# The first sum of weight blocks moves from VectorE to GpSimd, and ten steps of sixteen take seven products

## The chip, the cores and the metric

The kernel runs on one core of one Trainium2 chip. The metric is the time on the device, in microseconds (us), of one execution. PE is TensorE, DVE VectorE, ACT ScalarE, POOL GpSimd and SP SyncE. A "mixed unit" below is the piece of work that repeats 17 times in the kernel and that the change edits.

## The reference

With the sizes used here (sequence 256, width 4096, 32 heads of 128, one layer) the program is an attention branch and a final norm:

```python
h = x + attn_branch(rms_norm(x, norm_attn), w_in_attn, w_out_attn)
return rms_norm(h, final_norm)

def attn_branch(xn, w_in, w_out):
    proj = xn @ w_in                       # (256, 4096) @ (4096, 16384)
    q, k, v, g = jnp.split(proj, 4, axis=-1)
    o = stick_breaking_attention(to_heads(q), to_heads(k), to_heads(v))
    return (o * jax.nn.silu(g)) @ w_out    # (256, 4096) @ (4096, 4096)
```

Nearly all the arithmetic lies in the two products with `w_in` and `w_out`, in float32. The convolution branch of the reference file is not reached at this depth.

## The kernel before

**Products in three matmuls.** A float32 operand is split into a high part (rounded to the matmul's input form) and a low part (what is left). A product of two 128 x 128 by 128 x 512 operands is made of three matmuls into one PSUM bank: high by high, high by low, low by high. The weight tiles arrive by DMA into `raw` tiles (seven buffers); ACT casts a block to its high part `wh`, DVE subtracts it and leaves the low part `wl`. These two are made afresh for each block, since every weight is used once. Five buffers of two blocks and two of one block hold `wh` and `wl` between DVE and PE.

**Units and steps.** The output columns are worked off in units of four 512-column pieces (two row halves by two column groups). 15 of the 16 units over `w_in` and two of those over `w_out` are mixed units; the others (one plain unit of each matrix, and two single ones at the end) multiply in the plain way. A unit has 16 steps over the contraction; each step takes a 2 x 2 block of 128-row weight pieces against a 2 x 2 block of the input.

**Seven or eight products.** In a mixed unit a step whose number stands in `SEVEN` (line 42) uses a Strassen-Winograd scheme of seven products on seven forms of weights; the other steps use eight plain products. `SEVEN_PARTS` and `EIGHT_PARTS` (lines 67 and 73) list the parts. An eight-product step casts and splits four blocks (two `wl` rows of 128 x 1024). A seven-product step splits seven (three `wl` rows of 128 x 1024 and one of 128 x 512), because it also needs sums of weight blocks. One of these, called T3 in the code, is made by a DMA that adds while it writes (`add_block`, line 401, issued by POOL). The other three are made by `sums(q)` (line 424), in place in the two raw tiles `one` and `two`: `one0 = one0 - two0`, then `two1 = one0 + two1`, then `one1 = one0 + one1`. All three are `TENSOR_TENSOR` rows of 128 x 512 on DVE: in the rows of the order the first reads `raw_0<-raw_0,raw_1`, the second `raw_1<-raw_0,raw_1` and the third `raw_0<-raw_0`. The first waits until T3 has landed and the first part's `wl` is made from the old contents; the second waits also for the single-block part.

**Order.** Each engine runs its instructions in the order of the program, and this order is fixed when the program is built. A planner (`Plan`) walks through all the work with assumed costs; when an engine is free, `turn` (line 212) takes the ready item with the lowest key. Keys are places in the sequence of products (`first[n]` is when part n is first needed, in ns of assumed PE time). DVE's sums have the key of the part that needs them less 3000. POOL issues the adding DMAs, the writes of the heads' outputs to DRAM (`spill`) and the later reloads (`p`). Attention heads of one unit run between the products of the next one: `head` and `gate` add PE transposes and matmuls, ACT functions and DVE rows (`f`, `fl`, `a`, `gated`, `gl`); `combine` adds up the unit's banks on DVE.

All instructions that pass through the planner's engine wrapper are recorded at line 115, so groups are told apart by tile names.

Of the kernel before, what the change touches and what calls it, by code (L numbers as in the profile page):

```python
# [14 lines left out]
ALU = mybir.AluOpType  # L15
# [13 lines left out]
W = 2 * CW  # L29
# [9 lines left out]

SEVEN = (1,3,5,7,8,10,11,13,14)
RAW_BUFS = 7
PAIRS = 5
SINGLES = 2
# [41 lines left out]

def scalar_ns(n):
    return 98 + n / 1.2


def tensor_ns(n):
# [138 lines left out]
def kernel(  # L231
# [10 lines left out]
    nc = Plan(tc)  # L242
# [30 lines left out]
    for u, (kind, w, cols) in enumerate(units):  # L273
        for s in range(NS):
# [5 lines left out]
            else:  # L280
# [6 lines left out]
                else:  # L287
                    which = SEVEN_PARTS if s in (SEVEN) else EIGHT_PARTS
            for i, (k, place, prods) in enumerate(which):
# [24 lines left out]
    starts, ends, first, left, place_of = {}, {}, {}, {}, {}  # L314
# [12 lines left out]
    def place_at(u, s):  # L327

        u, s = u + int(s // NS), s % NS
        a = place_of[u, int(s)]  # L330
        b = place_of.get((u, int(s) + 1), place_of.get((u + 1, 0), a))
        return a + (b - a) * (s - int(s))

    def soon(c=4.0):
        return nc.here + 1e3 * c


    def dve(emit, n, key=None, **kw):
        n = n if isinstance(n, tuple) else (n,)
        cost = sum(vector_ns(m) for m in n) + 122 * (len(n) - 1)  # L340
        return nc.work("vector", cost, emit, soon() if key is None else key, **kw)

    def act(emit, n, key=None, **kw):
        n = n if isinstance(n, tuple) else (n,)
        cost = sum(scalar_ns(m) for m in n) + 100 * (len(n) - 1)
        return nc.work("scalar", cost, emit, soon() if key is None else key, **kw)
# [66 lines left out]
    def tile_done(*tile):  # L413
        tile_left[tile] -= 1
        if not tile_left[tile]:
            nc.give("raw")
# [7 lines left out]
    def sums(q):  # L424

        a, b, c, d = quad_parts[q]
        one, two = raw[q, 0], raw[q, 1]
        for k in range(2):
            tile_left[q, k] += 1

        def add(to, at_, f, g, key, op=ALU.add):
            return dve(
                lambda: nc.vector.tensor_tensor(out=to[:, :, at_, :], in0=f, in1=g, op=op), W,
                key - SUMS_AHEAD * 1e3,
            )

        yield nc.until(("lows", a), ("T3", q))
        yield add(one, 0, one[:, :, 0, :], two[:, :, 0, :], first[c], ALU.subtract)
        yield nc.until(("lows", b))
        yield add(two, 1, one[:, :, 0, :], two[:, :, 1, :], first[c])  # L440
        nc.tell(("sums", c))
        yield add(one, 1, one[:, :, 0, :], one[:, :, 1, :], first[d])
        nc.tell(("sums", d))
        for k in range(2):
            tile_done(q, k)

    def piece(n, c, there):

        p = parts[n]
        yield nc.until(*there)  # L450
        full = raw[p["tile"]][:, :, p["place"], :][:, :, c, :].rearrange("p i c n -> p c i n")
        h, l = (t[n][:, c, :].rearrange("p c (i n) -> p c i n", i=HG) for t in (wh, wl))
        size = (c.stop - c.start) * W
        key = first[n] - (AHEAD * 1e3 if p["seven"] and p["i"] < 2 else 0)
        yield act(lambda: nc.scalar.copy(h, full), size, key - 2.0 * 1e3)
        yield dve(lambda: minus(l, full, h), size, key)
        for k in range(c.start, c.stop):
            nc.tell(("low", n, k))
        low_done(n)

    def split(size, tag, bufs):
        for n, p in enumerate(parts):
            if p["size"] != size:
                continue
            q = p["quad"]
            yield nc.take(tag)
            t = p["tile"][1]
            if q:
                yield nc.until(("raw", q, t))
            wh[n] = wp.tile([P, size, W], F32R, tag=tag + "h", name=f"wh{n}", bufs=bufs)  # L470
            wl[n] = wp.tile([P, size, W], F32R, tag=tag + "l", name=f"wl{n}", bufs=bufs)
            cuts = [slice(k, k + 1) for k in range(KT)] if q == 0 else [slice(0, size)]
            lows_left[n] = len(cuts)
            if p["seven"] and p["i"] == 0:
                nc.start(sums(q))
            for c in cuts:
                if q == 0:
                    there = [("raw", q, t, c.start)]
                else:
                    there = [("sums", n)] if p["seven"] and p["i"] > 1 else [("raw", q, t)]  # L480
                nc.start(piece(n, c, there))
# [7 lines left out]
    def new_forms(i, what):  # L489
        n = len(SEVEN_FORMS if i in SEVEN else EIGHT_FORMS)  # L490
        h = sp.tile([P, n, P], F32R, tag=f"xh{i}", name=f"{what}h{i}")
        l = sp.tile([P, n, P], F32R, tag=f"xl{i}", name=f"{what}l{i}")
        forms[i] = h, l
        return h, l

    def both_parts(i, to, f, key):
        h, l = (t[:, to, :] for t in forms[i])
        n = (to.stop - to.start) * P
        yield act(lambda: nc.scalar.copy(h, f), n, key - 1e3)
        yield dve(lambda: minus(l, f, h), n, key)  # L500

    def sums_of(i, y, what, key):

        tt = nc.vector.tensor_tensor
        if i not in SEVEN:
            y4 = y.rearrange("p (a b) c -> p a b c", a=KT)
# [21 lines left out]
    def blocks_of(i):  # L528
# [8 lines left out]
        if i:  # L537
            yield moved("sync", lambda: nc.sync.dma_start(y, xT[i]), [KT * S], key - 1, hold=True)

            def scaled():  # L540
                for c in range(KT):
                    nc.scalar.activation(y[:, c, :], y[:, c, :], AF.Copy, scale=gain(c))
                nc.scalar.copy(h[:, 0:4, :], y4)

            yield act(scaled, (S, S, 2 * S), key - 2e3)
            yield dve(lambda: minus(l[:, 0:4, :], y4, h[:, 0:4, :]), 2 * S, key)
        else:
            for k in range(KT):
                yield moved("scalar", lambda: nc.scalar.dma_start(y[:, k, :], xT[i][:, k, :]), [S], key - 1,
                            hold=k == 1, after=k == 0 and (lambda: nc.tell("x0")) or None)  # L550
                if k == 0:
                    yield moved("scalar", lambda: nc.scalar.dma_start(gcol, gain_in), [KC], key - 1,
                                after=lambda: nc.tell("gain"))
            for c in range(KT):
                hc, lc = (t[:, 2 * c : 2 * c + 2, :].rearrange("p a b -> p (a b)") for t in (h, l))

                def two_parts():
                    nc.vector.tensor_scalar(out=hc, in0=y[:, c, :], scalar1=gain(c), scalar2=None, op0=ALU.mult)
                    nc.vector.scalar_tensor_tensor(
                        out=lc, in0=y[:, c, :], scalar=gain(c), in1=hc.bitcast(F32), op0=ALU.mult, op1=ALU.subtract  # L560
                    )

                yield dve(two_parts, (S, S), key)
# [25 lines left out]
    for _ in range(WARM):  # L589
# [8 lines left out]
        out=bound, in_=bound, compare_op=ALU.is_gt, fill=0.0, base=0,  # L598
# [6 lines left out]
        out=tri_f, in_=tri_f, compare_op=ALU.is_ge, fill=0.0, base=0, pattern=[[-1, P]], channel_multiplier=1,  # L605
# [321 lines left out]
    def blocks_of_heads(s):  # L927
# [12 lines left out]
        nc.give("gh")  # L940
        if s in SEVEN:
            key = min(place_at(OUT0, s + 1), place_of[OUT0 + 1, s] - 3e3)
# [7 lines left out]
    def again(s):  # L950

        yield nc.until(("used", LAST - 2, s), later_than(LAST - 2, s))
        y = yield from heads_of(s, soon(), slice(1, 2))
        yield from both_parts(s, slice(1, 2), y[:, 1:2, :], soon())
        nc.give("gh")
        nc.tell(("form", "r", s))
# [79 lines left out]
    def blocks_out(u, c):  # L1036

        for d in range(2):
            for t in range(NT):
                yield nc.until(("used", u, 2 * (NT * d + t)), ("C", u - 1))  # L1040
                if t == 0:
                    yield nc.take("gh")
                    yield load_gain(c + d)
                yield nc.take("gh")
                yield load_out(c + d, t)
                yield from block_out(c + d, t, hs[c + d, t])
                nc.give("gh")
            nc.give("gh")
# [110 lines left out]
    def products():  # L1159
        for g, (n, k) in enumerate(order):  # L1160
# [9 lines left out]
            else:  # L1170
                what = "r" if u > LAST - 2 and s in SEVEN else "p"
            if starts[u, b] == (n, k):
# [20 lines left out]
    for k, c in enumerate(range(0, NJ - 2, 2)):  # L1193
        if k:
            nc.start(mixed_h(U + k, c))
        nc.start(blocks_out(U + k + 1, c))
    for s in SEVEN:
        nc.start(again(s))
# [40 lines left out]
```

## Time and profile before

| quantity | value |
|---|---|
| three runs | 1757.85 us median (1756.26 to 1759.46) |
| span of the profiled execution | 1754.0 us |
| mean granted clock of PE | 0.997 |
| busy PE / DVE / ACT / POOL | 1736.9 / 1560.4 / 1166.4 / 295.7 us |
| DMA share in the 40 slices | 4 to 9 tenths, mostly 7 or 8 |
| moved by DMA | 405.86 MB |

For the profiled execution the page gives only the span, from its first to its last instruction. The median of the runs stands 3.85 us above it; this is what lies around the span. Busy times of pipelined engines overlap at the ends of rows, so the busy time of a group is the union of its rows, while the mean of one row is longer than the distance from one start to the next. A wait is written as waiter <- releaser.

### The profile page before, as it was taken

How to read it: one execution, taken by the hardware profiler on the slowest of the kernel's cores; microseconds unless marked ns; L12 is line 12 of the kernel's file. 1: busy time of each engine (PE TensorE's matmuls, PEld its weight loads, DVE VectorE, ACT ScalarE, POOL GpSimd, SP SyncE). 2: the span in 40 equal slices, each digit the busy share in tenths (PEclk: the TensorE clock that was granted, in tenths of full speed). 3: DMA queues.
4: the chain of work that ended last, by engine and by line, in shares of the span. 5: the costliest groups of instructions: out<-in, count | busy, mean ns of one | idle time of the engine just before them, and what ended most of it. 6: DMA issues, size and time to landing. Idle time of an engine off the chain costs nothing.

```text
span 1754.0 us, 24699 instructions
## 1 busy us (share of the span) xinstructions
PE 1736.9 (99%) x7806; PEld 1427.1 (81%) x7806; DVE 1560.4 (89%) x1971; ACT 1166.4 (67%) x1594; POOL 295.7 (17%) x364
## 2 busy tenths in 40 slices
PE   8999999999999999999999999999999999999997
PEld 6888888888888888888888888888888888888885
DVE  7889999999999999999999999999999997899963
ACT  7975767676767676767676767676767675666543
POOL 0012121111111121211111111111112111111100
PEclk9999999999999999999999999999999999999998
DMA  9968777777777878787878787878786877889874
GB/s 340 316 192 224 230 218 229 223 223 226 222 228 217 239 210 239 208 245 210 240 208 245 208 239 206 242 202 245 200 246 200 262 244 239 229 245 271 257 236 156
DMA packets 242867, 405.86 MB, mean 231 GB/s; under 512 B 27520, under 2 KB 67968, under 8 KB 242736
## 3 DMA queue, kind: packets, MB, share of 16 engines
q1 hardware_dynamic: 193968, 352.15, 60.8%
q0 software_dynamic: 47184, 49.76, 17.3%
q10 hardware_dynamic: 1584, 2.38, 0.4%
q8 instruction: 61, 1.00, 0.2%
q14 instruction: 70, 0.57, 0.1%
HBM read 396.05 MB, written 8.13 MB: 230 GB/s over the span
## 4 chain that ended last, share of the span: by engine, by line
PE 92%; DVE 3%; issue 2%; DMA 2%; ACT 1%; SPq 0%; ACTq 0%; DVEq 0%
PE acc L115 87%; PE z L115 2%; DVE wl L115 2%; PE o L115 2%; DMA raw<-in_w_in_dram 1%; PE tr L115 1%; ACT wh L115 1%; DVE raw L115 0%; ACT h L115 0%; SPq L115 0%; DMA xres<-in_x_dram 0%; DMA raw<-in_w_out_dram 0%; ACTq L115 0%; DVE gv_sb L115 0%; DVE h L115 0%
## 5 line engine op out<-in xcount | busy, mean ns | idle before, releaser
L115 ACT CAST wh<-raw 128x1024 fp32r<-128x1024 f32 (+1 forms) x948 | 886.1, 976 | 476.1 <-issue 173.3
L115 DVE TENSOR_TENSOR wl<-raw,wh 128x1024 fp32r<-128x1024 f32 (+1 forms) x948 | 1032.1, 1131 | 125.3 <-ACT wh L115 118.6
L115 PE MATMUL acc<-wh,sh 128*128 128x512 f32 x1913 | 762.6, 399 | 2.4 <-DVE sh L115 2.1
L115 PE MATMUL acc<-wh,sl 128*128 128x512 f32 x1913 | 746.2, 390 | 0.0
L115 PE MATMUL acc<-wl,sh 128*128 128x512 f32 x1913 | 744.9, 389 | 0.8 <-DVE wl L115 0.8
L115 PEld LDWEIGHTS acc<-wh,sh 128*128 128x128 f32 x1913 | 359.4, 188 | 77.3 <-DVE gv_sb L115 3.9
L115 PEld LDWEIGHTS acc<-wh,sl 128*128 128x128 f32 x1913 | 359.1, 188 | 76.9 <-DVE sl L115 0.8
L115 PEld LDWEIGHTS acc<-wl,sh 128*128 128x128 f32 x1913 | 359.7, 188 | 71.5 <-DVE wl L115 1.5
L115 POOL DMA_DIRECT2D raw<-in_w_in_dram x270 | 236.1, 987 | 1075.7 <-DMA raw<-in_w_in_dram 403.1
L115 DVE TENSOR_TENSOR raw<-raw,raw 128x512 f32<-128x512 f32 x306 | 210.3, 687 | 5.1
L115 PE MATMUL acc<-wh,oh 128*128 128x512 f32 x494 | 193.2, 391 | 0.0
L115 PE MATMUL acc<-wl,oh 128*128 128x512 f32 x494 | 192.4, 389 | 0.6 <-DVE wl L115 0.6
L115 PE MATMUL acc<-wh,ol 128*128 128x512 f32 x494 | 192.3, 389 | 0.0
L115 PEld LDWEIGHTS acc<-wl,oh 128*128 128x128 f32 x494 | 92.8, 188 | 20.5 <-DVE wl L115 1.2
L115 PEld LDWEIGHTS acc<-wh,oh 128*128 128x128 f32 x494 | 92.8, 188 | 19.3 <-DVE gv_sb L115 0.4
L115 PEld LDWEIGHTS acc<-wh,ol 128*128 128x128 f32 x494 | 92.7, 188 | 19.2
L115 DVE TENSOR_TENSOR raw<-raw 128x512 f32<-128x512 f32 x153 | 104.5, 683 | 0.0
L115 POOL DMA_DIRECT2D raw<-in_w_out_dram x36 | 31.6, 992 | 132.5 <-DMA raw<-in_w_out_dram 66.2
L115 ACT ACTIVATE f<-f 128x384 f32<-128x384 f32 x96 | 50.5, 526 | 3.0
L115 DVE SCALAR_TENSOR_TENSOR f<-z,f 128x384 f32<-128x384 f32 x32 | 17.8, 557 | 31.2 <-ACT f L115 31.2
L115 POOL DMA_DIRECT2D p<-spill x33 | 20.3, 696 | 129.6 <-DVE ol L115 94.0
L115 ACT ACTIVATE gl<-gl 128x512 f32<-128x512 f32 x48 | 30.0, 625 | 7.3 <-DVE gl L115 7.3
(90 smaller groups left out, 745.9 us busy)
## 6 DMA issues: line engine op xcount, KB each, us to landing
raw<-in_w_in_dram SPq DMA_DIRECT2D x1020, 256.0 KB, 4.6
raw<-in_w_out_dram SPq DMA_DIRECT2D x256, 256.0 KB, 3.9
raw<-in_w_in_dram POOLq DMA_DIRECT2D x270, 128.0 KB, 5.2
raw<-in_w_out_dram POOLq DMA_DIRECT2D x36, 128.0 KB, 5.6
xr<-in_x_dram SPq DMA_DIRECT2D x16, 256.0 KB, 5.2
xres<-in_x_dram SPq DMA_DIRECT2D x16, 256.0 KB, 5.6
xs<-in_xT_dram SPq DMA_DIRECT2D x15, 256.0 KB, 5.3
spill<-gated POOLq DMA_DIRECT2D x15, 256.0 KB, 3.9
```

The costliest lines, as they stand in the source:

```text
L115: return self.tc.keep_in_program_order(getattr(self.engine, name)(*args, **kw))
```

## The change

Two things change. The first of the three sums of a seven-product step is issued on GpSimd by a new helper `pool_add`, with its own assumed cost and a key 25 us ahead of the part that needs it; the second and third sums stay on DVE. And `SEVEN` becomes another set of ten steps instead of nine. The set also decides which of the input's forms are made (seven forms for a step in `SEVEN`, six for another, once per matrix) and which heads are reloaded for them.

```diff
-SEVEN = (1,3,5,7,8,10,11,13,14)
+SEVEN = (1, 2, 4, 5, 7, 8, 10, 11, 13, 14)
...
+def pool_ns(n):
+    return 200 + 2.2 * n
...
+    def pool_add(to, f, g, key, op=ALU.add):
+        return nc.work(
+            "gpsimd", pool_ns(W), lambda: nc.gpsimd.tensor_tensor(out=to, in0=f, in1=g, op=op), key
+        )
...
         yield nc.until(("lows", a), ("T3", q))
-        yield add(one, 0, one[:, :, 0, :], two[:, :, 0, :], first[c], ALU.subtract)
+        yield pool_add(one[:, :, 0, :], one[:, :, 0, :], two[:, :, 0, :], first[c] - 2.5e4, ALU.subtract)
         yield nc.until(("lows", b))
         yield add(two, 1, one[:, :, 0, :], two[:, :, 1, :], first[c])
         nc.tell(("sums", c))
```

The rows of the two programs show what moves. Below is DVE in the seventh mixed unit around its step 8, with the numbers of the tiles: `raw120_0` and `raw120_1` are the two raw tiles of that step, `wl356` in the program before and `wl370` in the changed one are the low part of its first two blocks. Before:

```order
L115 TENSOR_TENSOR wl356_6271<-raw120_0_6142,wh356_6270 128x1024 [waits DMAHW1_49,DMAHW0_49,Activation_49]
L115 TENSOR_TENSOR raw120_0_6142<-raw120_0_6142,raw120_1_6097 128x2x256 [waits DMASW3_49,DMASW2_49,DVE_49]
L115 TENSOR_TENSOR raw120_1_6097<-raw120_0_6142,raw120_1_6097 128x2x256 [waits DVE_49]
L115 TENSOR_TENSOR raw120_0_6142<-raw120_0_6142 128x2x256
L115 TENSOR_TENSOR wl358_6291<-raw120_1_6097,wh358_6290 128x1024 [waits Activation_49]
L115 TENSOR_TENSOR wl359_6302<-raw120_0_6142,wh359_6301 128x1024 [waits Activation_49]
```

And with the change, at the same step:

```order
L119 TENSOR_TENSOR wl370_6346<-raw120_0_6245,wh370_6345 128x1024 [waits DMAHW1_49,DMAHW0_49,Activation_49]
L119 TENSOR_TENSOR raw120_1_6187<-raw120_0_6245,raw120_1_6187 128x2x256 [waits Pool_49]
L119 TENSOR_TENSOR raw120_0_6245<-raw120_0_6245 128x2x256 [waits DVE_49]
L119 TENSOR_TENSOR wl372_6366<-raw120_1_6187,wh372_6365 128x1024 [waits DMASW1_49,DMASW0_49,Activation_49]
L119 TENSOR_TENSOR wl373_6375<-raw120_0_6245,wh373_6374 128x1024 [waits Activation_49]
```

The row between the low part and the second sum is gone from DVE, and the second sum now waits for POOL. The sum on POOL itself cannot start before the low part is done, because it overwrites what that row reads. Of the 170 steps of seven products in the changed program, 41 have no DVE row between the low part and the second sum, 51 have one, 32 two, 31 three and 15 four.

On POOL, for the same stretch (steps 119 to 126 are steps 7 to 14 of that unit; a `DMA raw` row is T3 of that step, in two pieces). Before:

```order
L115 DMA raw119_1_6055<-in_w_in_dram 128x256 x2
L115 DMA raw120_1_6097<-in_w_in_dram 128x256 x2
L115 DMA raw122_1_6192<-in_w_in_dram 128x256 x2
L115 DMA spill6_6265<-gated6_6088 128x512
L115 DMA raw123_1_6276<-in_w_in_dram 128x256 x2
```

With the change:

```order
L119 TENSOR_TENSOR raw119_0_6178<-raw119_0_6178,raw119_1_6118 128x2x256
L119 DMA spill6_6327<-gated6_6141 128x512
L119 DMA raw122_1_6274<-in_w_in_dram 128x256 x2
L119 TENSOR_TENSOR raw120_0_6245<-raw120_0_6245,raw120_1_6187 128x2x256
L119 DMA raw123_1_6348<-in_w_in_dram 128x256 x2
L119 TENSOR_TENSOR raw122_0_6339<-raw122_0_6339,raw122_1_6274 128x2x256
L119 DMA raw125_1_6424<-in_w_in_dram 128x256 x2
L119 TENSOR_TENSOR raw123_0_6400<-raw123_0_6400,raw123_1_6348 128x2x256
L119 DMA raw126_1_6492<-in_w_in_dram 128x256 x2
L119 TENSOR_TENSOR raw125_0_6480<-raw125_0_6480,raw125_1_6424 128x2x256
L119 TENSOR_TENSOR raw126_0_6539<-raw126_0_6539,raw126_1_6492 128x2x256
```

The adding DMAs now stand behind sums that wait for DVE: T3 of step 126 is issued after the sum of step 123, and used two sums later. In the whole program PE has 51 matmul rows of products fewer, DVE 75 rows fewer, ACT 37 rows more, and POOL 170 sums and 36 DMA rows more.

## The prediction

> **What bounds the kernel now.** I read the engines' shares first, then the chain of waits, then the waits by engine, and then the mixed units by windows. The shares and the chain's summary:
>
> ```profile
> PE 1736.9 (99%) x7806; PEld 1427.1 (81%) x7806; DVE 1560.4 (89%) x1971; ACT 1166.4 (67%) x1594; POOL 295.7 (17%) x364
> PE 92%; DVE 3%; issue 2%; DMA 2%; ACT 1%; SPq 0%; ACTq 0%; DVEq 0%
> 654.40 51.03 PE acc L115 x225
> ```
>
> PE carries 92% of the chain. The third line, from the chain in order of time, is a stretch without a break: 225 matmuls start in 51.03 us, one every 0.2268 us. The 389 ns that a row of such a matmul lasts is pipelined and is no price. A product of three matmuls costs 0.680 us.
>
> The view of waits says how near DVE is:
>
> ```profile
> PE acc L115 <- DVE wl L115: 1.4, 2, 0.8
> DVE wl L115 <- ACT wh L115: 118.6, 182, 3.5
> DVE f L115 <- ACT f L115: 31.2, 30, 1.4
> ```
>
> PE hardly ever waits for a low part. DVE's waits for `wh` are those of an engine that is ahead, since ACT's casts wait for buffers that PE frees. The waits in the heads (`f`, 31.2 us over 15 units, 2.1 each) would stay if DVE fell behind.
>
> The windows put numbers on one mixed unit over `w_in` (its length is half of the 173.7 us after which the chain repeats), and on the two over `w_out`:
>
> ```profile
> core 0: us, PE busy (x) PEld busy (x) DVE busy (x) ACT busy (x) POOL busy (x), PEclk, DMA share, GB/s
> 480.72:567.50 86.78, 86.78 (x393) 71.46 (x393) 79.92 (x96) 58.28 (x78) 15.77 (x19) 1.00 0.78 223
> 567.50:654.40 86.90, 86.90 (x395) 71.47 (x394) 80.02 (x96) 58.94 (x79) 16.84 (x20) 1.00 0.79 225
> sum 521.00, PE 520.99 PEld 428.79 DVE 479.82 ACT 351.61 POOL 97.88; mean PE 86.83 PEld 71.47 DVE 79.97 ACT 58.60 POOL 16.31
> sum 160.00, PE 160.00 PEld 132.50 DVE 139.97 ACT 95.57 POOL 29.75; mean PE 80.00 PEld 66.25 DVE 69.98 ACT 47.79 POOL 14.88
> ```
>
> The first sum is of six units, the second of 160 us that cover the two units over `w_out`. PE is full at a granted clock of 1.00. DVE works 79.97 of 86.83 us: 6.9 us of reserve, of which 2.1 are the heads' waits. Over `w_out` it works 70.0 of 80. So PE is the bound, and DVE is the engine that becomes it if its work grows by some 5 us per unit.
>
> **What the change takes from PE.** 17 mixed units lose one product each: 17 x 0.680 = 11.6 us. This is the whole gain if nothing else binds: 86.83 becomes 86.15 per unit.
>
> **What it does to DVE's own work.** The prices:
>
> ```profile
> L115 DVE TENSOR_TENSOR wl<-raw,wh 128x1024 fp32r<-128x1024 f32 x791 | 935.7, 1220 | 120.2 <-ACT wh L115 113.5 <-DMA raw<-in_w_in_dram 2.2 <-DMA xres<-in_x_dram 1.5
> L115 DVE TENSOR_TENSOR raw<-raw,raw 128x512 f32<-128x512 f32 x306 | 210.3, 687 | 5.1
> L115 DVE TENSOR_TENSOR wl<-raw,wh 128x512 fp32r<-128x512 f32 x157 | 107.2, 683 | 5.1 <-ACT wh L115 5.1
> ```
>
> A `wl` row of 1024 takes 935.7/791 = 1.18 us, a sum 0.69, a `wl` row of 512 0.68. Nine first sums leave: -6.2. The tenth step of seven adds one `wl` of 1024, one of 512 and two sums: 1.18 + 0.68 + 1.37 = +3.2. So 79.97 becomes 77.0 us per unit, in 86.15. By work alone DVE is relieved. ACT gets two casts more per unit (under 2 us on 58.6 of 86.8) and the DMA two adding transfers; at shares of 0.67 and 0.79 I cost both at nothing, covered by PE. The input's further forms are made once per matrix, under 4 us of DVE in all, in its reserve.
>
> **What POOL's sum costs.** The trace has no two-input row on POOL. The nearest:
>
> ```profile
> L115 POOL TENSOR_SCALAR_AFFINE_SELECT bound<-bound 128x128 f32<-128x128 f32 x1 | 0.3, 292 | 0.1
> L1226 POOL MEMSET const-bfloat16-1.0<- 128x1 bf16 x1 | 0.1, 101 | 0.0
> L115 POOL DMA_DIRECT2D raw<-in_w_in_dram x270 | 236.1, 987 | 1075.7 <-DMA raw<-in_w_in_dram 403.1 <-DVE raw L115 226.3 <-DVE wl L115 210.2
> ```
>
> 101 ns for one element is the fixed part; 292 - 101 = 191 ns for 128 elements of one input makes 0.76 us for 512, so 0.87 us is the lower end. If two inputs take twice as long per element, 0.10 + 1.53 = 1.63 is the upper. I take the middle, 1.2 us. The Trainium skill (GPSIMD Engine Reference, section 3.1) gives 4497 ns for 2048 elements of a two-input float32 sum, as an estimate 1.1 us for 512; by that figure the forecast below would be 15 us lower.
>
> **What DVE loses by it.** The second sum cannot start before POOL's sum, and POOL's cannot start before the first low part. One row shows the way from DVE to POOL:
>
> ```profile
> 655.76 0.42 DVE L115 TENSOR_TENSOR gated<-o,gated 128x256 f32<-128x256 f32 x1
> 656.48 0.58 POOL L115 DMA_DIRECT2D spill<-gated  x1 [2.29 <-DVE gated L115]
> ```
>
> From 656.18 to 656.48, 0.30 us. So 1.5 us pass from low part to second sum, and what DVE has between them is at most what the order put there: nothing at 41 of the 170 places, one row (0.6 to 1.2 us) at 51. The lower end is that DVE runs those rows at full speed beside POOL: 1.5 less what stands between, averaged over the places of the order with a row of 1024 at 1.13 (the distance of starts) and one of 512 at 0.60, is 6.3 us per ten steps. Then DVE needs 77.0 + 2.1 + 6.3 = 85.4 of 86.15 and PE still binds, by a hair.
>
> The upper end is that nothing of DVE runs while POOL sums, because DVE's rows here are nearly all of two inputs from the same memory that POOL is reading twice. Then each step costs the whole sum: 10 x 1.2 = 12.0, and DVE needs 77.0 + 2.1 + 12.0 = 91.1 us per unit. No row of this trace has a POOL instruction that reads beside a DVE row of two inputs, so the trace doesn't choose. I take the upper end, since the lower one needs two engines with four input streams to run side by side at full speed, and already leaves DVE without reserve. I leave out the 0.30 us where DVE has nothing between, against the few rows with one input from PSUM that might run beside POOL.
>
> The Trainium skill (SBUF — State Buffer, "Who interferes with whom") has a rule that speaks against the change: a vector instruction with two SBUF inputs contends with a GpSimd instruction that reads SBUF, and whichever starts second is blocked until the other ends. By that rule the upper end holds; no run here shows it so far.
>
> **The sum.** Over `w_in`: 91.1 - 86.83 = +4.3 per unit, times 15 = +64. Over `w_out` DVE needs 70.0 - 3.0 + 12.0 = 79.0 of 80 less 0.7: PE still binds, two units gain 1.4. Together +63 on the profiled 1754.0 us, that is 1817 in span and, with the 3.85 us around it, **1820 us** against the median. With the sum at 0.87 us DVE needs 87.8 and the time is 1757.85 + 15 x 1.0 - 1.4 = 1772; at 1.63 it needs 95.4 over `w_in`, and over `w_out` 83.3 of 80: 1757.85 + 15 x 8.6 + 2 x 3.3 = 1893.
>
> **Rivals.** *The two engines run side by side* (0.25). DVE needs 85.4 and PE keeps 86.15. All 17 units gain 0.68: 1746 us, faster. For it speaks that the work alone falls by 3 us per unit; against it that 0.7 us of reserve in 86 must absorb every late cast.
>
> *They overlap in part* (0.21). POOL's sum costs DVE some 0.9 us, 9 per unit: DVE needs 88.1, +1.3 over 15 units, less 1.4: 1776 us. From 0.8 us per sum on DVE binds; below it the first rival holds.
>
> *T3 comes late* (0.04). POOL issues in order, and T3 of a later step now stands behind a sum that waits for DVE (step 126's behind the sum of step 123). The price: two issues of 0.987 us and a median landing of 5.2 us:
>
> ```profile
> raw<-in_w_in_dram POOLq DMA_DIRECT2D x270, 128.0 KB, 5.2
> ```
>
> 7.2 us after the sum of step 123 it is there; it is wanted three steps later, after 7 + 8 + 7 products, 15.0 us. It decides only if the sums on POOL run 7.8 us late against PE. Then a wait of perhaps 2 us at five places of a unit would add 10 us per unit: 1757.85 + 150 = 1908. The reserve makes it unlikely.
>
> That the seven-product steps don't come is excluded by the order: 51 matmuls are gone.
>
> **How the numbers follow.** The forecast (DVE loses POOL's whole sum) gets 0.50 and 1820 us, with its own range of 1790 to 1870 for a sum of 1.0 to 1.5 us. The range over all cases reaches down to the first rival, 1745, and up to 1870, and leaves out the long sum and the late T3. A measurement of this kernel can tell about 0.2% (3.5 us) from no change. Faster 0.25 (the first rival), the same 0.05 (the part of the second between 1754 and 1761), slower 0.70.
>
> **What would show it.** In the changed profile the windows of a mixed unit should be 90 to 92 us long, with DVE without idle time apart from waits for POOL, and PE waiting for `wl`. The waits should list DVE raw <- POOL raw, about 170 times, some tenths to 1.5 us each. POOL's sums should last 1.0 to 1.5 us, and the DVE rows that meet them should be longer than 1220 or 687 ns, or start later. It is wrong if PE is still full and the unit is 86.2 us; then DVE's rows keep their length beside POOL's. If DVE is idle while POOL waits for `DMA raw`, T3 is the cause. POOL's own busy time should rise by 170 x 1.2 + 34 x 0.99, some 240 us.

## The result, and the profile after

The changed kernel takes 1834.71 us (median of 4 runs, 1833.76 to 1836.04) against 1757.05 us for the kernel before in the same measurement: a ratio of 1.0441 with a 95% interval of 1.0427 to 1.0456. It is slower by 77.7 us, though TensorE has 51 matmuls less to do.

The shares and the chain's summary of the changed kernel, as shown above of the one before:

```profile
span 1834.0 us, 25044 instructions
PE 1752.7 (96%) x7755; PEld 1411.7 (77%) x7755; DVE 1540.0 (84%) x1896; ACT 1186.3 (65%) x1631; POOL 637.8 (35%) x570
DVE 28%; PE 25%; issue 22%; ACT 15%; POOL 6%; DMA 4%; ACTq 0%; SPq 0%; DVEq 0%; POOLq 0%
```

PE's part of the chain fell from 92% to 25%. What took its place is no single engine: the chain now goes to and fro between DVE, ACT, POOL and PE. DVE is less busy than before (84%, it was 89%) and yet holds up more.

The windows of two mixed units over `w_in` (columns as above), then of all 15 of them and of the two over `w_out`:

```profile
487.15:578.20 91.05, 87.62 (x391) 70.68 (x391) 78.03 (x92) 59.80 (x79) 35.95 (x31) 1.00 0.74 215
578.20:669.28 91.08, 87.41 (x392) 70.35 (x391) 78.02 (x92) 59.64 (x79) 36.68 (x31) 1.00 0.76 219
96.90:1464.10 1367.20, 1312.87 (x5848) 1058.78 (x5847) 1169.39 (x1362) 897.46 (x1189) 539.53 (x462) 1.00 0.75 216
1559.90:1735.30 175.40, 166.22 (x710) 131.28 (x709) 155.49 (x171) 102.11 (x129) 68.97 (x57) 1.00 0.79 231
```

And the same two stretches of the kernel before:

```profile
97.00:1399.30 1302.30, 1301.98 (x5895) 1071.71 (x5893) 1195.98 (x1435) 880.85 (x1159) 242.73 (x284) 1.00 0.78 224
1492.20:1655.10 162.90, 162.30 (x716) 133.81 (x715) 152.50 (x178) 99.81 (x124) 29.65 (x35) 1.00 0.86 250
```

A unit over `w_in` went from 86.8 to 91.1 us, the 15 of them from 1302.3 to 1367.2 (+64.9), the two over `w_out` from 162.9 to 175.4 (+12.5). These make 77.4 of the 80.0 us by which the span grew. PE's clock stayed at 1.00.

The waits of the changed kernel, in us in total, times and longest:

```profile
DVE raw L119 <- POOL raw L119: 157.8, 124, 1.5
PEld acc L119 <- DVE wl L119: 49.5, 70, 1.4
PEld tr L119 <- DVE qk_sb L119: 25.1, 14, 2.4
PE acc L119 <- DVE wl L119: 22.9, 44, 1.1
PE tr L119 <- DVE qk_sb L119: 20.1, 14, 2.1
PE tr L119 <- DVE gated L119: 16.9, 15, 1.3
```

DVE's second sum waits for POOL in 124 of 170 steps, 157.8 us in all. That is not all due to the meeting of the two engines. Taken sum by sum from the trace, 87 us of it would be there with each of POOL's sums at the 1.28 us that it takes alone: DVE had nothing else in its order and waited for the hand-over (to POOL and back). The other 71 us stand behind sums that lasted longer. PE, which hardly waited before, waits for low parts, and at the transposes of the attention heads for DVE's rows `qk_sb` and `gated`, which stand behind those waits in DVE's order.

The groups of both engines' rows, and the lengths of POOL's sum (min/median/max, from the view by tile):

```profile
L119 DVE TENSOR_TENSOR wl<-raw,wh 128x1024 fp32r<-128x1024 f32 x808 | 963.0, 1236 | 82.7 <-ACT wh L119 82.3
L119 DVE TENSOR_TENSOR wl<-raw,wh 128x512 fp32r<-128x512 f32 x174 | 127.5, 745 | 4.1 <-ACT wh L119 4.1
L119 POOL TENSOR_TENSOR raw<-raw,raw x170: 1277/1662/3405, 94.5 to 1722.7; 128x512 f32<-128x512 f32 x170
```

The sum takes 1.28 us when it is let alone, but its median is 1.66 and its longest 3.4. DVE's `wl` rows grew a little on average (1236 ns after 1220, 745 after 683). One piece of the order of time shows how the two meet; the first lines are DVE's, the last is POOL's:

```profile
568.77 2.35 DVE L119 TENSOR_TENSOR wl<-raw,wh 128x1024 fp32r<-128x1024 f32 x2
571.04 0.41 DVE L119 TENSOR_TENSOR a<-a,bound 128x256 f32<-128x256 f32 x1
571.37 0.68 DVE L119 TENSOR_TENSOR wl<-raw,wh 128x512 fp32r<-128x512 f32 x1
573.22 0.69 DVE L119 TENSOR_TENSOR raw<-raw,raw 128x512 f32<-128x512 f32 x1 [1.17 <-POOL raw L119]
570.07 3.12 POOL L119 TENSOR_TENSOR raw<-raw,raw 128x512 f32<-128x512 f32 x1 [5.72 <-DVE wl L119]
```

POOL's sum starts at 570.07 while DVE runs `wl` and `a` and `wl` without a gap until 572.05. It ends at 573.19, 1.14 us after DVE's last row, which is nearly all the time that it needs. While DVE streamed, it got nowhere; then DVE, with nothing left but the row that waits for it, stood still for 1.17 us.

The other sums agree. Of the 170, 42 meet no DVE row whose inputs both lie in SBUF, the memory of the tiles, for more than 0.1 us (PE's results lie in another one, PSUM), and these last 1.28 to 1.30 us. The other 128 lie beside such rows for 138.7 us in all, and the two engines' rows are longer than alone by 93.4 us (POOL) and 30.3 us (DVE), together 123.7: all of the time side by side but for 0.12 us per sum.

### The profile page after: what moved, and what is told of

It is laid out like the page before. It is cut to its first block, busy times and chain, and to the rows that moved or that the text cites. A ratio compares the mean times of both kernels' runs of the same rounds, so it can differ in the third digit from the quotient of the medians.

```text
span 1834.0 us, 25044 instructions
## 1 busy us (share of the span) xinstructions
PE 1752.7 (96%) x7755; PEld 1411.7 (77%) x7755; DVE 1540.0 (84%) x1896; ACT 1186.3 (65%) x1631; POOL 637.8 (35%) x570
## 3 DMA queue, kind: packets, MB, share of 16 engines
q1 hardware_dynamic: 193968, 352.15, 56.7%
## 4 chain that ended last, share of the span: by engine, by line
DVE 28%; PE 25%; issue 22%; ACT 15%; POOL 6%; DMA 4%; ACTq 0%; SPq 0%; DVEq 0%; POOLq 0%
PE acc L119 23%; DVE wl L119 20%; ACT wh L119 10%; POOL raw L119 6%; DVE raw L119 3%; ACT f L119 2%; DMA raw<-in_w_in_dram 2%; ACT gl L119 1%; DVE gv_sb L119 1%; DMA raw<-in_w_out_dram 1%; DVE qk_sb L119 1%; PE tr L119 1%; PE z L119 1%; DVE gl L119 1%; DVE h L119 0%
## 5 line engine op out<-in xcount | busy, mean ns | idle before, releaser
L119 ACT CAST wh<-raw 128x1024 fp32r<-128x1024 f32 (+1 forms) x982 | 900.2, 971 | 535.5 <-PE acc L119 168.4
L119 DVE TENSOR_TENSOR wl<-raw,wh 128x1024 fp32r<-128x1024 f32 (+1 forms) x982 | 1082.1, 1149 | 86.8 <-ACT wh L119 86.4
L119 POOL TENSOR_TENSOR raw<-raw,raw 128x512 f32<-128x512 f32 x170 | 310.9, 1829 | 594.8 <-DVE wl L119 518.0
L119 PEld LDWEIGHTS acc<-wh,sh 128*128 128x128 f32 x1898 | 356.9, 188 | 78.6 <-ACT gv_sb L119 5.1
L119 POOL DMA_DIRECT2D raw<-in_w_in_dram x300 | 266.0, 1014 | 356.6 <-DMA raw<-in_w_in_dram 164.0
L119 DVE TENSOR_TENSOR raw<-raw,raw 128x512 f32<-128x512 f32 x170 | 117.0, 688 | 157.8 <-POOL raw L119 157.8
L119 DVE TENSOR_TENSOR raw<-raw 128x512 f32<-128x512 f32 x170 | 116.0, 682 | 0.0
L119 POOL DMA_DIRECT2D p<-spill x35 | 19.3, 562 | 112.6 <-DVE ol L119 66.8
L119 PE MATMUL tr<-ident,qk_sb 128*128 128x128 f32 x128 | 23.1, 285 | 37.0 <-DVE qk_sb L119 20.1
L119 PEld LDWEIGHTS tr<-ident,qk_sb 128*128 128x128 f32 x128 | 14.1, 140 | 49.4 <-DVE qk_sb L119 25.1
```

The lines of the kernel that those rows point to most:

```text
L119: return self.tc.keep_in_program_order(getattr(self.engine, name)(*args, **kw))
```

## The experiments

Theory A is that POOL's reading and DVE's rows of two SBUF inputs exclude each other; theory B that only the hand-over between the engines costs time; theory C that the pattern is to blame.

| run | us | ratio to before, 95% interval |
|---|---|---|
| ten steps, all sums on VectorE | 1758.77 | 1.0017 (1.0008 to 1.0026) |
| nine steps, first sum on GpSimd | 1820.13 | 1.0366 (1.0352 to 1.0380) |
| planned 1.7 us later | 1786.70 | 1.0173 (1.0159 to 1.0187) |
| planned 3.4 us later | 1842.49 | 1.0479 (1.0451 to 1.0506) |
| GpSimd writes only, ten steps | 1734.97 | 0.9882 (0.9866 to 0.9899) |
| GpSimd writes only, nine steps | 1746.95 | 0.9940 (0.9922 to 0.9958) |
| sum of 384 of 512 columns | 1798.56 | 1.0238 (1.0223 to 1.0254) |
| 272 idle sums beside the old kernel | 1990.56 | 1.1337 (1.1319 to 1.1355) |
| 272 idle writes beside the old kernel | 1756.27 | 0.9997 (0.9988 to 1.0007) |
| GpSimd sum in every second step | 1812.02 | 1.0312 (1.0294 to 1.0331) |
| in steps 5, 7, 8, 10, 11 | 1819.65 | 1.0358 (1.0343 to 1.0373) |
| in steps 1, 2, 4, 13, 14 | 1779.94 | 1.0131 (1.0113 to 1.0149) |

### The two halves of the change apart

The changed kernel with the first sum back on VectorE:

```diff
-        yield pool_add(one[:, :, 0, :], one[:, :, 0, :], two[:, :, 0, :], first[c] - 2.5e4, ALU.subtract)
+        yield add(one, 0, one[:, :, 0, :], two[:, :, 0, :], first[c], ALU.subtract)
```

> The ten-step pattern with all three sums on VectorE. Theory A (the GpSimd sum and VectorE's two-input rows exclude each other, so each sum costs VectorE about its whole 1.2 us): without the GpSimd sums VectorE needs 79.97 + 3.2 + 0.7 + 2.1 = 86.0 us of the 86.15 that TensorE needs per unit, so 1746 to 1756 us. Theory B (only the hand-over between the engines costs time, they run side by side): the same, 1746 to 1756. Theory C (the pattern is to blame: two seven-product steps in a row, five times per unit, come too fast for VectorE or the adding DMA): 1800 us or more.

And the changed kernel with the old steps:

```diff
-SEVEN = (1, 2, 4, 5, 7, 8, 10, 11, 13, 14)
+SEVEN = (1,3,5,7,8,10,11,13,14)
```

> The first sum on GpSimd with the old nine steps. Theory A: nine sums cost VectorE some 10 us per unit against 6.2 us of work that leaves it; VectorE then needs 86 to 88 of the 86.83 us of a unit, so 1757 to 1785 us. Theory B: much the same hand-overs (0.75 us missing per sum at 1.6 us of way there and back), 6.8 per unit against 6.2 gained: 1757 to 1765. Theory C: 1757, as before.

The pattern alone takes 1758.77 us, 0.17% over the kernel before and 3 us over the range expected. The move alone takes 1820.13, 35 us over the 1757 to 1785 of theory A, so the sum of DVE's work from which that range came misses something (more on it below). The move to POOL is what costs all the same: with the ten steps it adds 75.9 us (1834.7 less 1758.8), with the nine 64.4. Theory C falls. The pattern costs nothing that matters and gains nothing either; it uses up on DVE what it saves on PE (DVE is busy for 1609.7 us in place of 1560.4, and PE waits 10.7 us for low parts in place of 1.4). PE's share of the chain is 38% in this run, at the time of the kernel before: a share of the chain doesn't measure a loss.

### Does a read on GpSimd stop VectorE, with nobody waiting?

To the kernel before, one sum per step of a mixed unit was added on POOL, from a constant tile to a tile that nobody reads; in a second run, three constants written to that tile:

```diff
+    flat = cp.tile([P, 1, P], F32, name="flat")
+    scratch = cp.tile([P, 4, P], F32, name="scratch")
+    nc.gpsimd.memset(flat, 1.0)
+    twice = flat.broadcast_to([P, 4, P])
...
+    def extra(n):
+        def emit():
+            nc.gpsimd.tensor_tensor(out=scratch, in0=twice, in1=twice, op=ALU.add)
+        yield nc.work("gpsimd", 1300, emit, first[n] - 2e4)
...
+            if p["i"] == 0 and 0 < p["u"] and q < len(quads) - 32:
+                nc.start(extra(n))
```

> The kernel before, with one more GpSimd sum of 128x512 per step of a mixed unit (272 in all) from a constant tile to a tile that nobody reads. Nothing waits for it, so no hand-over. Theory A: VectorE's two-input rows that start beside a sum last up to 1.2 us longer (up to 2.4 us for 1024 elements), the sums themselves last up to some us; VectorE loses more than its 4.8 us of reserve per unit, so the time is 1775 to 1850 us. Theory B: no VectorE row changes its length, the time is 1755 to 1762 us.

> As the run with idle sums, but each sum is three constants of 128x512 written to the same tile that nobody reads (some 1.5 us, at least as long on GpSimd's queue): it only writes. Theory A: no VectorE row changes, 1755 to 1765 us. Theory that it's GpSimd's queue that counts (adding DMAs that are issued late behind the extra work): as slow as the run with idle sums. Theory B: 1755 to 1762 us.

1990.56 against 1756.27 us. DVE's and POOL's rows in the run with sums, then in the run with writes (by tile for DVE, by group for POOL):

```profile
L115 DVE TENSOR_TENSOR wl<-raw,wh x948: 676/1220/3443, 4.8 to 1970.0; 128x1024 fp32r<-128x1024 f32 x151, 128x512 fp32r<-128x512 f32 x39
L115 POOL TENSOR_TENSOR scratch<-flat 128x512 f32<-128x512 f32 x272 | 462.2, 1699 | 10.3
```

```profile
L115 DVE TENSOR_TENSOR wl<-raw,wh x948: 683/1220/1234, 4.7 to 1731.4; 128x1024 fp32r<-128x1024 f32 x151, 128x512 fp32r<-128x512 f32 x39
L115 POOL MEMSET scratch<- 128x512 f32 x816 | 502.0, 615 | 38.6
```

Writes kept POOL as busy as the sums (502 us and 462), ahead of the same adding DMAs, and no `wl` row was longer than 1.23 us. Sums that read made `wl` rows last up to 3.4 us, and the kernel 233.7 us longer (1990.56 less 1756.87 for the kernel before in the same measurement), 0.86 us for each of the 272. DVE's busy time rose by 264 us, from 1560.4 to 1824.7. Nothing waited for the sums. So theory B can't be the whole, and POOL's queue isn't the cause. (PE's granted clock was 0.982 in the run with sums and 0.998 in the one with writes; as an estimate from these two, that makes at most 32 of the 234 us.) The size was beyond the expected 1775 to 1850: I had counted on DVE's idle time to take up much of it.

The same run shows which DVE rows are held up. Both of these have two inputs; `acc` lies in PSUM, `gv_sb` and `gl` lie in SBUF:

```profile
L115 DVE TENSOR_TENSOR gv_sb<-acc,gv_sb x30: 678/680/687, 192.8 to 1621.3; 128x512 f32<-128x512 f32 x30
L115 DVE TENSOR_TENSOR gv_sb<-gv_sb,gl x16: 678/680/2757, 105.5 to 1640.4; 128x512 f32<-128x512 f32 x16
```

Of the rows with an input in PSUM (`gv_sb`, `qk_sb` and `f<-z,f`), 34 lay beside a sum for most of their length, and none grew. Rows with both inputs in SBUF did.

### The same hand-over, with and without a read

In the changed kernel, POOL's sum was replaced by a constant that it writes to the whole tile, and in another run it was cut to 384 of its 512 columns; the order of DVE's rows around it is the same in all three:

```diff
-            "gpsimd", pool_ns(W), lambda: nc.gpsimd.tensor_tensor(out=to, in0=f, in1=g, op=op), key
+            "gpsimd", pool_ns(W), lambda: nc.gpsimd.memset(to, 0.01), key
...
-        yield pool_add(one[:, :, 0, :], one[:, :, 0, :], two[:, :, 0, :], first[c] - 2.5e4, ALU.subtract)
+        yield pool_add(one[:, :, :, :], one[:, :, 0, :], two[:, :, 0, :], first[c] - 2.5e4, ALU.subtract)
```

```diff
-        yield pool_add(one[:, :, 0, :], one[:, :, 0, :], two[:, :, 0, :], first[c] - 2.5e4, ALU.subtract)
+        yield pool_add(one[:, :, 0, 0:192], one[:, :, 0, 0:192], two[:, :, 0, 0:192], first[c] - 2.5e4, ALU.subtract)
```

> The changed kernel with its order, but in place of the first sum GpSimd writes a constant over the whole tile (1024 elements per partition, some 0.9 to 1.0 us by the two MEMSET rows of the trace before), and reads nothing: the first sum is left out. Same waits for the low part before it and by the second sum behind it. Theory A (GpSimd's reading excludes VectorE's two-input rows): no row is lengthened on either engine, only the bare hand-over stays (0.47 us missing per sum at 1.3 us of way, 4.7 per unit), VectorE needs 77 + 2 + 4.7 = 84 us and the time is 1746 to 1775 us. Theory B (hand-over alone): as the kernel with a shorter GpSimd sum of the same length, within 8 us.

> The changed kernel with its order, but the first sum is made for 384 of the 512 columns only (the rest keeps the old values): 0.9 to 1.0 us alone by the 1.287 us of the whole sum. It reads two inputs and is as long as the write in the run with the constant. Theory A: GpSimd still starves or holds up VectorE, the loss shrinks with the sum's length, some 0.3 us per sum and 10 sums per unit: 1785 to 1805 us, clearly over the run that only writes; sums with VectorE rows beside them last 1.3 us and more. Theory B: equal to the run that only writes, within 8 us.

POOL's rows of the two runs, and DVE's wait for them:

```profile
L119 POOL MEMSET raw<- x170: 951/956/1538, 94.1 to 1619.1; 128x1024 f32 x170
DVE raw L119 <- POOL raw L119: 56.7, 68, 1.2
```

```profile
L119 POOL TENSOR_TENSOR raw<-raw,raw x170: 1002/1389/3122, 94.4 to 1685.7; 128x384 f32<-128x384 f32 x170
DVE raw L119 <- POOL raw L119: 130.6, 132, 1.2
```

Both kernels leave out the sum or a quarter of it; they serve to measure. Two POOL rows of nearly one length (0.951 and 1.002 us alone), in the same place of the same order, and 63.6 us between the kernels: 1734.97 and 1798.56. The write stays at its length, the sum's median is 1.39. Of the wait behind the sum, 56.7 us are bare hand-over (the run with the write), and they cost nothing: PE is full in that run (85.54 of 85.54 us of a unit). Theory B falls here. Theory A's range for the part sum is met (1785 to 1805); the run that writes came out 11 us below its range, which the next experiment explains. From the part sum to the whole one it is another 36.2 us (1798.56 to 1834.71). That step lengthens the hand-over and the meeting at once, and no run takes them apart.

### How much VectorE already cost the kernel before

> The old nine steps, with a constant written by GpSimd in place of the first sum (which is left out), as in the run with ten steps that took 1735 us. It asks what the tenth step is worth where VectorE has no part in it. Theory D (the kernel before lost some 10 us to VectorE under a TensorE that the profile shows as full): 1735 + 11.6 = 1744 to 1749 us, clearly under the kernel before. Theory E (the kernel before was bound by TensorE alone, and the run with ten steps gained from something else): 1755 to 1759 us.

The run that only writes, with the nine old steps: 1746.95 us. The tenth step is worth 12.0 us (1746.95 less 1734.97, or 11.4 with each taken against the kernel before of its own measurement; the prediction had 11.6), and with the same matmuls as the kernel before the time is 10.5 us shorter, since the first sums are gone from DVE. So the kernel before lost 10 us to DVE (to its work or to the order that came with it), though its windows showed PE busy for 1301.98 of 1302.30 us. Theory D holds.

### More room for the hand-over

The planner was told that the sum takes 1.7 us longer, and in another run 3.4 us (3600 in place of 1900):

```diff
 def pool_ns(n):
-    return 200 + 2.2 * n
+    return 1900 + 2.2 * n
```

> The changed kernel, but the planner is told that a GpSimd sum takes 1.7 us longer, so it puts other VectorE rows between the low part and the second sum: 2.3 us of them on average in place of 1.1, and at 169 of 170 places at least one row. Theory B (hand-over only): the 1.6 us of way are covered nearly everywhere (0.10 us missing per sum in place of 0.67), TensorE binds again and the time falls to 1746 to 1775 us. Theory A (exclusion): the rows put between don't run beside the sum; GpSimd's sum lasts longer (mean over 2.2 us in place of 1.83) or VectorE's rows do, VectorE loses 1 to 1.3 us per sum as before, and the time stays at 1815 to 1850 us.

> The changed kernel with the planner told that GpSimd's sum takes 3.4 us longer than in the change (1.7 longer gave 1787 us). More VectorE rows stand between, 3.3 us on average. Theory A: the hand-over has nothing more to give, and what is left is the exclusion: sums last 2 us and more, VectorE rows stay lengthened, 1770 to 1795 us. Theory B: VectorE's waits for GpSimd go to nothing and the time to 1735 to 1750 us.

1786.70 and 1842.49: neither theory's range holds. With 1.7 us, the wait for POOL falls to 63.1 us, and the cost comes back in part as longer rows; with 3.4, they are longer still. Three groups of DVE's rows in the first run, then the `wl` rows of the second with PE's waits:

```profile
L119 DVE TENSOR_TENSOR wl<-raw,wh 128x1024 fp32r<-128x1024 f32 x808 | 994.8, 1274 | 49.6 <-ACT wh L119 47.5 <-DMA raw<-in_w_out_dram 1.5 <-DMA raw<-in_w_in_dram 0.4
L119 DVE TENSOR_TENSOR fl<-f,fh 128x384 fp32r<-128x384 f32 x32 | 33.0, 1032 | 0.0
L119 DVE TENSOR_TENSOR a<-a,bound 128x256 f32<-128x256 f32 x32 | 31.1, 972 | 0.0
```

```profile
L119 DVE TENSOR_TENSOR wl<-raw,wh 128x1024 fp32r<-128x1024 f32 x808 | 1039.4, 1322 | 99.8 <-ACT wh L119 96.9 <-DMA raw<-in_w_in_dram 1.9
PE acc L119 <- DVE wl L119: 60.8, 72, 2.3
```

A mean of 1274 ns is 54 over the undisturbed 1220: 44 us over 808 rows. The heads' rows `fl` and `a` (548 and 414 ns in the changed kernel) add 33 us. With the 63.1 of waiting that is 140 us, where the changed kernel loses 157.8 + 13 + 11 = 182 (its rows of 1024 are 16 ns longer, those of 512 62). So room helped, 48 us of the 78, and more than half of what it left on DVE (77 of 140) is the exclusion in its other form. With 3.4 us more PE waits 60.8 us for low parts, and DVE's `wl` rows of 1024 alone are 82 us longer. An order that hides the hand-over has to be paid for elsewhere; how much of that wait comes from the later place of the sums and how much from the longer rows, the runs don't separate.

### Where in the unit the sums stand

> The ten steps, with the first sum on GpSimd in every second of them (1, 4, 7, 10, 13) and on VectorE in the others. Theory A (a sum costs VectorE 1.05 us on GpSimd and 0.60 to 0.69 on itself): half way between the run with all sums on VectorE (1759) and the changed kernel (1835), 1785 to 1805 us. If it is the crowding of two such sums in a row that costs the time, it lies within 10 us of 1759.

```diff
-        yield pool_add(one[:, :, 0, :], one[:, :, 0, :], two[:, :, 0, :], first[c] - 2.5e4, ALU.subtract)
+        if parts[a]["s"] in SEVEN[::2]:
+            yield pool_add(one[:, :, 0, :], one[:, :, 0, :], two[:, :, 0, :], first[c] - 2.5e4, ALU.subtract)
+        else:
+            yield add(one, 0, one[:, :, 0, :], two[:, :, 0, :], first[c], ALU.subtract)
```

1812.02 us: half of the sums cost 53 of the 76 us, more than their number. That is 7 us over theory A's range, and no two sums in a row were needed for it, so crowding of two such sums isn't what costs the time either. Since PE waited at the heads' transposes, two more runs put the five sums away from the heads' rows or next to them (the condition is then `in (5, 7, 8, 10, 11)` or `in (1, 2, 4, 13, 14)`):

> Ten steps, with the first sum on GpSimd in steps 5, 7, 8, 10 and 11 and on VectorE in 1, 2, 4, 13 and 14: as many GpSimd sums as in the run with every second (1812 us), but none ahead of the rows that the attention heads wait for (the combined sums of a unit, behind steps 13 and 14, and the gating of the first head, behind steps 1 to 4). Theory F (where a GpSimd sum stands decides: VectorE is in order, and a late head row stops TensorE at the transposes): TensorE's waits at the transposes, 47 us in the changed kernel, fall under 15 us, and the time is 1770 to 1800 us. Theory G (only the number of such sums counts): 1805 to 1820 us.

> The other half: GpSimd sums in steps 1, 2, 4, 13 and 14, VectorE sums in the rest. Theory F: the transposes wait 30 us or more and the time is 1805 to 1830 us, at least 15 us over its counterpart. Theory G: 1805 to 1820 us, within 8 us of its counterpart.

1819.65 and 1779.94: place does decide, 39.7 us at the same number, but the other way round. PE's waits in the run away from the heads, then next to them:

```profile
PE acc L119 <- DVE wl L119: 29.6, 54, 1.9
PE tr L119 <- DVE gated L119: 7.6, 8, 1.0
PE tr L119 <- DVE qk_sb L119: 6.3, 7, 0.9
```

```profile
PE tr L119 <- DVE gated L119: 11.7, 15, 1.1
PE acc L119 <- DVE wl L119: 5.4, 8, 1.5
PE tr L119 <- DVE qk_sb L119: 1.5, 7, 0.2
```

Both theories fall. Away from the heads the transposes do wait less than in the changed kernel (13.9 us after 37.0), as theory F has it, but next to the heads they wait as little (13.2, where it expects 30 or more). What differs is PE's wait for low parts, 29.6 and 5.4 us, and on DVE the wait for POOL, 78.6 and 50.9 us: the median sum on POOL takes 2.14 us away from the heads and 1.66 next to them. Why the sums of steps 5, 7, 8, 10 and 11 are held up longer stays open.

## Why the prediction was right, and where it was off

**The way and the cause.** Forecast was 1820 us, because DVE loses about the whole of POOL's sum in each step. Measured are 1834.7 us, and the cause is that one: reads on POOL and rows of two SBUF inputs on DVE don't run together (the idle sums, the part sum against the write, the lengths of the sums). The trace agrees with the rule of the Trainium skill (SBUF — State Buffer, "Who interferes with whom") that the prediction named as speaking against the change: 3.4 us for a row of 1.2 beside reads, 1.23 at most beside writes. The trace goes further in one point: the sum at 570.07 was kept back beyond the end of the row that ran when it started, until the whole train of rows was over.

**POOL's sum**, taken as 1.2 us between 0.87 and 1.63: 1.28 us alone. The two lengths measured, 1.002 us for 384 columns and 1.277 for 512, make 2.15 ns per element and 0.18 us besides, where the two ends of the guess had 1.49 and 2.98 ns and 0.10 us. That the middle came so near is luck. POOL's busy time rose by 342 us and not by 240, since the sums that meet DVE's rows last longer (1.83 us on average).

**DVE's own work**, 77.0 us per unit by the sum of what leaves and what comes: 77.07 in the run that only writes (mean of two units of 85.58 us).

**What DVE loses**, 12.0 us per unit: 182 us over 17 units, 10.7. The form was not the expected one. I expected longer DVE rows and a DVE without idle time apart from its waits for POOL. The `wl` rows are 24 us longer in all, and 157.8 us are waits: it is mostly POOL that is held up, and DVE pays when it reaches the row that needs the sum. Of the 182 us, 87 are bare hand-over, of which the prediction left out a part, and 95 come from the meeting; in both forms POOL's sum gets done while DVE's rows don't run. So DVE is idle 13.0 of 91.1 us and still the reason. The unit over `w_in` came out at 91.1, as forecast, but the parts of it differ: 78.0 busy, some 9.5 of wait for POOL, and 3.5 of other waits, where the prediction had 77.0, 12.0 and 2.1.

**The sum itself** is weaker than its hit. With nine steps the same sum gives 79.97 - 6.2 + 2.1 + 9 x 1.2 = 86.7 of 86.83 us, no loss at all, and the nine-step run lost 64.4 us. In that run DVE is busy for only 1513.2 of 1820.9 us, and PE still waits for single rows of it (19.3 us at the transposes for `qk_sb`, 13.6 for `fl`, 9.9 for low parts); a sum of totals doesn't hold such waits. So the way and the cause were foreseen, and that the unit over `w_in` came out to the tenth is in part luck. The 3.85 us around the span were too many as well: each run's time stands 1.65 to 2.18 us above its own span.

**The term that was mis-sized** is the one over `w_out`: "PE still binds, two units gain 1.4". They lost 12.5, and this is nearly all of the 14.7 us between 1820 and 1834.7. The price was taken from 160 us of windows that begin 52 us before the first of these units, in the plain unit, where DVE has less to do. In the units themselves DVE is busy for 152.5 of 162.9 us, 76.3 per unit and not 70.0. With that, the same sum gives 76.3 - 3.0 + 12.0 = 85.3 us per unit, where the unit took 81.45 before: a loss of some 4 us, the right sign, and two thirds of the 6.25 measured.

**The rivals.** Side by side (1746 us): refuted by the measured time and by the run with 384 columns against the one that writes. Its floor was wrong too: PE can do the ten steps in 1735 us; what it was worked out from, a TensorE that is the bound at 1757, hid 10 us that DVE cost. Overlap in part (0.9 us a sum, 1776 us): the changed kernel loses 182/170 = 1.07 us a sum, between that and the 1.2 of the forecast. (By its own sum DVE would bind from 0.7 us per sum on, not from 0.8.) The size alone doesn't decide between them; the lengths of the sums do, since the two engines' rows run side by side for no more than 0.12 us per sum. Late T3: in the run that writes, with ten steps, the adding DMAs stand in the same order behind POOL rows that wait for DVE, and it takes 1735 us. In the changed kernel DVE and ACT wait 10.3 us for the DMAs of `raw`, in the one before 16.9.

**What stays open** is how a loss on DVE becomes a loss of the kernel. The two don't go together from run to run. With 1.7 us more of planned room DVE loses 140 us and the kernel takes 1786.7; with a GpSimd sum in every second step DVE loses some 83 (71.0 of waiting and 12 of longer rows), and the kernel takes 1812.0. The two places where PE stops are seen (low parts of a step that needs the sums, and the heads' transposes), but which order would be best was not found. No version with a true sum on GpSimd beat the kernel before; the ones that beat it leave the sum out.

## What to carry to other kernels

Before an operation is moved off a nearly full VectorE, ask what the move takes from VectorE while the other engine works: here a sum that cost it 0.69 us cost it 1.07 us once GpSimd did it, about half of it as hand-over. Beside a VectorE that streams two inputs from SBUF, sums on GpSimd that read SBUF cost 0.86 us each here even with nobody waiting; as much time in writes cost nothing. A sum of busy times holds totals only: it came out right for ten steps and missed 64 us with nine. And take the price of a stage from windows that begin and end with it.

## What the runs showed of the hardware that was not expected

- A GpSimd sum can be held up by a whole train of VectorE rows: 1.28 us alone, up to 3.4 in the changed kernel. In the other direction a VectorE row of 1.22 us lasted up to 3.4 us beside idle sums. Rows with an input in PSUM kept their length there (0.687 us at most for `gv_sb<-acc,gv_sb`).
- 272 constant writes of three rows each, 502 us of GpSimd's time, changed the kernel by a ratio of 0.9997 (0.9988 to 1.0007).
- A TensorE that the windows show as full (1301.98 of 1302.30 us) had some 10 us per run in it that a lighter VectorE gave back.
